# Mixer data in idle places of the raw-weight buffer, and layer 1's gate weights and column sums at other points of the program

## The chip, the cores and the metric

The kernel runs on one core of one Trainium2 chip. The metric is the device time of one execution in microseconds (us); lower is better. The kernel before takes 1125.44 us, the median of three runs (1125.43 to 1125.86).

## What is computed

A trunk of two layers on x of 512 tokens by 1024 channels, all in float32. Each layer is x + mixer(rmsnorm(x)), then x + mlp(rmsnorm(x)); a last rmsnorm ends the trunk. The MLP is `relu(h @ w1)**2 @ w2` with 4096 hidden channels.

- Layer 0's mixer has two halves. Differential attention: 4 heads, each with two softmaxes over 64-wide queries and keys, `p1 - lam * p2`, times v, normed per head. And pooling: 4 groups of 128 channels u, each `r = mean of the last w tokens - u` with w = 2, 4, 8, 16, times a 128x128 matrix. The eight results of 128 channels go through one output projection.
- Layer 1's mixer is gated linear attention, 4 heads with 128-wide keys and 256-wide values: `log_a = log_sigmoid(h @ w_low @ w_up + b) / 16` (the low rank is 16), a running sum of log_a per chunk gives the decays, then scores, state and output; the output is normed per head, multiplied by `silu(h @ w_g)` and projected.

## The kernel before

**Layout and matmuls.** Activations are kept with channels on the partitions: eight tiles of 128x512. A float32 product is made of three matmuls in a reduced format: a tensor is split into a high part (ScalarE, a copy) and a low part (VectorE, the difference), and hi x hi, lo x hi and hi x lo are added in one PSUM bank (L143 to L145, called by `proj_T`). `split_w` makes the two parts of a weight tile (L121 on ACT, L122 on DVE), `split_scaled` those of a normed activation (L175, L176), `split` those of a mixer's output (L181, L182). There are four buffers each for high and low weight parts, so a split waits until TensorE has read the tile four tiles before.

**Norms.** The norm's factor `rb` isn't applied ahead of a projection but behind it, when the result leaves PSUM. `Norm.add` adds the squares of the eight tiles (L232 on ACT, L241 on DVE); `col_sums` splits the sum (L197, L198) and adds over the partitions with two matmuls (L199, L200); `rsqrt` takes logarithm and exponential (L211, L212) and one Newton step (L204 to L206).

**Memory.** Weights come from HBM in loads of 1 MB into `raws`, 24 places of 512 columns: a ring of two loads (places 0 to 7) in the mixers, of five (0 to 19) in the MLPs, where places 20 to 23 hold a temporary `t2` of the weights. In layer 1's mixer places 8 to 11 hold states and 12 to 19 the values. Most other tensors are tiles of the pool `row` (54 of 128x512) or `tmp` (4). PSUM has eight banks under two tags, `mm` and `ax`, four each.

**Order.** A scheduler puts the instructions of each engine in a fixed order when the program is built, by priority (`soon()` raises it) and by when tiles come free. Engines then run in order and wait for each other by semaphores; all loads of weights are issued by SyncE (SP) in order too.

**Around the change.** In layer 0, q and k (L302), v (L355) and in layer 1 the gates g (L841) are rows. The pooling's u lies in two places of its own, with three more for its running sums (L398, L403). After layer 0's MLP, layer 1 begins: the low-rank gate weights `wgk` and the second gate matrix `wup` are loaded (L622, L624) and split (L637, L638, L641, L642); `psg` gathers the gate's column sums in 16 matmuls (L651), eight ahead of each half of head 0's q and k. Then `rb`; `gkf` (L659), its split (L660, L661), the second gate product for four heads (L665), `log_sigmoid` (L668 to L677, between two loads of ACT's tables, L674 and L679), running sums (L683), and head 0's q leaves PSUM (L699). At the mixer's end `gts` are taken through SiLU (L845), multiplied into the outputs (L846) and split (L181, L182) for the output projection (L421 adds its result to x).

Of the kernel before, what the change touches and what calls it, by code (L numbers as in the profile page):

```python
# [9 lines left out]
F32 = mybir.dt.float32  # L10
F32R = mybir.dt.float32r
U8 = mybir.dt.uint8
AF = mybir.ActivationFunctionType
ALU = mybir.AluOpType
AX = mybir.AxisListType

P = 128
S = 512
D = 1024
KB = D // P  # L20
# [15 lines left out]
def trunk(ctx: ExitStack, tc: tile.TileContext, xT, par, lvl, lam4, wqk0, wu0, wv0, poolw, wo0,  # L36
          wgk, wup, wqk1, wv1, wg1, wo1, w1a, w2a, w1b, w2b, gfin, out):
    nc = tc.nc
    V, A, G, PE = nc.vector, nc.scalar, nc.gpsimd, nc.tensor
# [10 lines left out]
    raws = T([P, 24 * S], "wraw", 1)  # L50
    ring = {}

    def turn(name, bufs):
        ring[name] = ring.get(name, -1) + 1
        return ring[name] % bufs

    def row(n=S, dt=F32):
        return T([P, n], "row", 54, dt)

    row8 = row16 = tmp2 = row  # L60


    def row_u(sums=True):
        c0 = 8 * S + (2 + turn("us", 3) if sums else turn("u", 2)) * (16 + S)
        return raws[:, c0:c0 + 16 + S]

    def row_state():
# [3 lines left out]
    mlp = [False]  # L71

    def tmp(n=S, dt=F32):
        if not mlp[0] and turn("tmp", 3) == 2:
            return row(n, dt)
        return T([P, n], "tmp", 4, dt)

    def PS(tag, shape=(P, S)):
        cnt[0] += 1
        return pp.tile(list(shape), F32, tag=tag, bufs=4, name=f"ps{tag}_{cnt[0]}")  # L80
# [5 lines left out]
    def soon(n=300):  # L86
        return tc.high_priority(n)
# [173 lines left out]
    act = []  # L261
# [9 lines left out]
    for kb in range(KB):  # L271
        c = slice(kb * P, (kb + 1) * P)
# [24 lines left out]
    def qk_heads(h):  # L297
        for j in range(2):
            ps = ps0[j] if h == 0 else proj_T(st.next(), act)
            t = row8()  # L300
            with soon():
                V.tensor_tensor(t, ps, rb, ALU.mult)  # L302
            qk[h, j] = t
# [46 lines left out]
    def values():  # L350
        r0 = per_token(rb)
        for t, ps in enumerate(proj_tok(Stream(wv0), act)):
            vt = row8()
            with soon():
                A.activation(vt, ps, AF.Copy, scale=r0[:, t:t + 1])  # L355
            v.append(vt)
# [35 lines left out]
    for i, g in enumerate((3, 2, 1, 0)):  # L392
        w = POOL_W[g]
        ps = proj_T(st.next(), act)
        u = row_u(False)
        G.memset(u[:, 0:16], 0.0)
        with soon():
            V.tensor_tensor(u[:, 16:], ps, rb, ALU.mult)  # L398
        s, step = u, 1
        while step < w:  # L400
            s2 = row_u()
            G.memset(s2[:, 0:16], 0.0)
            V.tensor_tensor(s2[:, 16:], s[:, 16:], s[:, 16 - step:16 + S - step], ALU.add)  # L403
            s, step = s2, 2 * step
        r = tmp2()
        V.scalar_tensor_tensor(out=r[:, 16:], in0=s[:, 32:], scalar=1.0 / w, in1=u[:, 32:], op0=ALU.mult,
                               op1=ALU.subtract)
        V.tensor_tensor(r[:, 0:16], s[:, 16:32], prm[:, C_ICNT + 16 * g:C_ICNT + 16 * (g + 1)], ALU.mult)
        V.tensor_tensor(r[:, 0:16], r[:, 0:16], u[:, 16:32], ALU.subtract)
        psy = PS("ax")  # L410
        PE.matmul(psy, pw[:, g, :], r, start=True, stop=True)
        cat[NH + i] = split_scaled(psy, prm[:, C_PSC + g:C_PSC + g + 1], (row16(dt=F32R), row16(dt=F32R)))

    def add_out(arr, src, col):

        st = Stream(arr)
        n, nxt = Norm(), []
        for f in range(KB):
            ps = proj_T(st.next(), src)
            with soon():  # L420
                V.tensor_tensor(x[f], x[f], ps, ALU.add)  # L421
                nxt.append(split_scaled(x[f], prm[:, col + f:col + f + 1]))
            n.add(x[f])
        return nxt, n

    def ffn(w1, w2, act, nrm, col):

# [15 lines left out]
        for c in range(4):  # L443
# [85 lines left out]
            def gather(t, nh, ps, first=False):  # L529
                with soon():  # L530
                    if first and c == 0 and not final:
                        acc[t][nh] = row8()
                        A.activation(acc[t][nh], ps, AF.Copy)
                    else:
                        V.tensor_tensor(acc[t][nh], acc[t][nh], shaped(ps), ALU.add)
# [7 lines left out]
            for n, (ps, first, t0, nh) in enumerate(plan):  # L543
                if n + 2 < 7:
                    w.append(prep(n + 2))
                product(n, w[n], ps, first)
                for t in range(2):
                    gather(t0 + t, nh, ps[t], n in (0, 2, 3))
            if c < 3:
                product(6, w[6], X, False)  # L550
                for t in range(2):
                    gather(2 + t, 0, X[t], True)
# [65 lines left out]
        nc.sync.dma_start(lf, lvl[:, i * S:(i + 1) * S])  # L618
        V.tensor_copy(lv[:, 4 * i:4 * i + 4, :].rearrange("p a b -> p (a b)"), lf)
    act, nrm = ffn(w1a, w2a, act, nrm, C_MIX1)  # L620
    gkr = row().rearrange("p (k a c) -> p k a c", k=KB, a=4)
    nc.sync.dma_start(gkr, wgk)  # L622
    wur = row()[0:96, :]
    nc.sync.dma_start(wur, wup)  # L624
    mlp[0] = False


    with soon(800):
        smask = row8()
        G.memset(smask, 1.0)  # L630
        G.memset(smask.rearrange("p (c t) -> p c t", t=P)[:, :, 0:1], 0.0)


        gk2 = [row8(dt=F32R).rearrange("p (k a b) -> p k a b", k=4, a=4) for _ in range(2)]
        for i in range(2):
            src = gkr[:, 4 * i:4 * i + 4, :, :]
            A.activation(gk2[i][:, :, :, 0:16], src, AF.Copy)  # L637
            V.tensor_tensor(gk2[i][:, :, :, 16:32], src, gk2[i][:, :, :, 0:16].bitcast(F32), ALU.subtract)  # L638

        wu = row8(dt=F32R)  # L640
        A.activation(wu[0:96, :], wur[0:96, :], AF.Copy)  # L641
        V.tensor_tensor(wu[64:96, :], wur[64:96, :], wu[64:96, :].bitcast(F32), ALU.subtract)  # L642

    psg = PS("mm")
    st = Stream(wqk1)
    wq0 = [st.next(), st.next()]
    psq0 = [PS("mm"), PS("mm")]
    for kbs in ((4, 5, 6, 7), (0, 1, 2, 3)):
        for kb in kbs:
            for j in range(2):  # L650
                PE.matmul(psg, gk2[kb // 4][:, kb % 4, :, :].rearrange("p a b -> p (a b)"), act[kb][j],  # L651
                          start=kb == 4 and j == 0, stop=kb == 3 and j == 1)
        for j in range(2):
            proj_T(wq0[j], act, ps=psq0[j], kbs=kbs, first=4, last=3)
    rb = nrm.rb()

    gkf = tmp2()
    gkl = row8(dt=F32R)
# [117 lines left out]

    def values1(half):
        for t, ps in enumerate(proj_tok(vst, act)):
            vt = raws[:, (12 + 4 * half + t) * S:(13 + 4 * half + t) * S]
            with soon():  # L780
                A.activation(vt, ps, AF.Copy, scale=r1[:, t:t + 1])
            vv[t][half] = vt
# [53 lines left out]
    gts = []  # L836
    for f in range(KB):
        ps = proj_T(st.next(), act)
        gt = row8()
        with soon():  # L840
            V.tensor_tensor(gt, ps, rb, ALU.mult)  # L841
        gts.append(gt)
# [95 lines left out]
```

## Time and profile before

| | |
|---|---|
| median of three runs | 1125.44 us |
| profiled execution, its own time | 1124.67 us |
| its span | 1122.9 us |
| busy: TensorE / VectorE / ScalarE | 1077.9 / 827.7 / 530.9 us |
| longest waits of TensorE | 11.0 us at L651, 7.9 us at L143 (for L699), 4.9 us at L143 (for L181) |
| granted clock, mean | 0.985 |

The profile is of one execution; its times are us from the span's start. A busy TensorE is at work or has a matmul in its pipe: in an unbroken run matmuls of 512 columns start every 0.227 us though one lasts 0.39. A line number is that of the helper that issued the instruction, so that L143 stands for every projection.

### The profile page before, as it was taken

Reading aid. Unit: us, or ns where it says so; the run is one execution under the profiler, and the core shown is the slowest. Engines: PE = TensorE matmul, PEld = TensorE weight load, DVE = VectorE, ACT = ScalarE, POOL = GpSimd, SP = SyncE. Lnnn points to the kernel's source line nnn. Section 1 sums busy time; section 2 is a strip of 40 time slices with the busy share of each in tenths; the row PEclk is TensorE's granted clock in tenths of the full one; section 3 lists DMA queues with packets and bytes.
Section 4 is the critical chain, followed back from the end, with each engine's and each line's share of the span. In section 5 each row is a group of like instructions: output and inputs, shape, how many; then the busy total and the mean of one; then the engine's idle time right before and its main releaser. Section 6 shows DMA issues by size and latency. Waiting matters only on the chain.

```text
span 1122.9 us, 12904 instructions
## 1 busy us (share of the span) xinstructions
PE 1077.9 (96%) x4968; PEld 867.5 (77%) x4968; DVE 827.7 (74%) x1234; ACT 530.9 (47%) x884; POOL 2.1 (0%) x20
## 2 busy tenths in 40 slices
PE   7999979999999999997879999999999999999996
PEld 5676658888888888886657788878888888888885
DVE  7757657695596696698588977556697597596696
ACT  6444525554443453445364546454554453453453
POOL 0000000000000000000000000000000000000000
PEclk9999989999999999999889999999999999999998
DMA  7221133305305206103211224222304305306102
GB/s 251 95 85 66 42 118 132 113 1 188 113 1 207 93 1 225 37 8 122 75 38 38 76 76 151 79 109 76 113 19 182 118 1 187 113 1 217 45 1 76
DMA packets 17917, 103.52 MB, mean 92 GB/s; under 512 B 2016, under 2 KB 3040, under 8 KB 6208
## 3 DMA queue, kind: packets, MB, share of 16 engines
q1 hardware_dynamic: 17712, 102.67, 25.5%
q8 instruction: 39, 0.64, 0.2%
q14 instruction: 22, 0.18, 0.1%
q10 hardware_dynamic: 144, 0.03, 0.0%
HBM read 100.59 MB, written 2.10 MB: 91 GB/s over the span
## 4 chain that ended last, share of the span: by engine, by line
PE 92%; DVE 3%; ACT 3%; DMA 1%; issue 0%; SPq 0%; DVEq 0%; ACTq 0%
PE psmm L143 15%; PE psmm L144 15%; PE psmm L145 14%; PE psmm L525 6%; PE psmm L527 6%; PE psmm L526 6%; PE psax L143 3%; PE psax L145 3%; PE psax L144 3%; PE psax L525 3%; PE psax L527 3%; PE psax L526 2%; PE psmm L169 2%; PE psmm L167 2%; PE psmm L168 2%; PE psax L316 1%
## 5 line engine op out<-in xcount | busy, mean ns | idle before, releaser
L121 ACT ACTIVATE wh<-wraw 128x1024 fp32r<-128x1024 f32 x230 | 243.6, 1061 | 420.5 <-PE psmm L144 181.5
L122 DVE TENSOR_TENSOR wl<-wraw,wh 128x1024 fp32r<-128x1024 f32 x230 | 280.3, 1221 | 82.6 <-ACT wh L121 82.0
L143 PE MATMUL psmm<-row,wh 128*128 128x512 f32 x736 | 290.9, 398 | 20.9 <-ACT row L181 7.9
L144 PE MATMUL psmm<-row,wh 128*128 128x512 f32 x736 | 290.8, 396 | 0.7 <-DVE row L182 0.7
L145 PE MATMUL psmm<-row,wl 128*128 128x512 f32 x736 | 290.7, 396 | 0.0
L143 PEld LDWEIGHTS psmm<-row,wh 128*128 128x128 f32 x736 | 139.5, 190 | 54.3 <-ACT row L181 9.3
L144 PEld LDWEIGHTS psmm<-row,wh 128*128 128x128 f32 x736 | 140.0, 190 | 33.4 <-issue 3.4
L145 PEld LDWEIGHTS psmm<-row,wl 128*128 128x128 f32 x736 | 139.6, 190 | 30.6 <-issue 2.0
L525 PE MATMUL psmm<-wh,row 128*128 128x512 f32 x320 | 124.6, 389 | 0.0
L526 PE MATMUL psmm<-wh,row 128*128 128x512 f32 x320 | 124.5, 389 | 0.0
L527 PE MATMUL psmm<-wl,row 128*128 128x512 f32 x320 | 124.5, 389 | 0.0
L500 DVE TENSOR_TENSOR wraw<-wraw 128x1024 f32<-128x1024 f32 x64 | 77.1, 1216 | 0.3
L452 DVE TENSOR_TENSOR row<-row,row 128x512 fp32r<-128x512 f32 x112 | 74.8, 682 | 0.3 <-ACT row L451 0.3
L527 PEld LDWEIGHTS psmm<-wl,row 128*128 128x128 f32 x320 | 60.1, 188 | 12.6
L526 PEld LDWEIGHTS psmm<-wh,row 128*128 128x128 f32 x320 | 60.1, 188 | 12.4
L525 PEld LDWEIGHTS psmm<-wh,row 128*128 128x128 f32 x320 | 60.1, 188 | 12.4
L451 ACT ACTIVATE row<-row 128x512 fp32r<-128x512 f32 x112 | 65.7, 618 | 5.3 <-DVE row L478 5.3
L466 DVE SCALAR_TENSOR_TENSOR tmp<-psmm,rb 128x512 f32<-128x512 f32 x48 | 32.9, 685 | 45.7 <-PE psmm L145 45.7
L471 ACT ACTIVATE row<-tmp 128x256 f32<-128x256 f32 x128 | 45.8, 405 | 10.9 <-DVE tmp L466 10.6
L145 PE MATMUL psax<-row,wl 128*128 128x512 f32 x128 | 49.8, 389 | 0.0
L144 PE MATMUL psax<-row,wh 128*128 128x512 f32 x128 | 49.8, 389 | 0.0
L527 PE MATMUL psax<-wl,row 128*128 128x512 f32 x128 | 49.8, 389 | 0.0
(231 smaller groups left out, 1306.5 us busy)
## 6 DMA issues: line engine op xcount, KB each, us to landing
wraw<-in_w1a SPq DMA_DIRECT2D x16, 1024.0 KB, 4.8
wraw<-in_w2a SPq DMA_DIRECT2D x16, 1024.0 KB, 4.8
wraw<-in_w2b SPq DMA_DIRECT2D x16, 1024.0 KB, 4.8
wraw<-in_w1b SPq DMA_DIRECT2D x16, 1024.0 KB, 4.8
wraw<-in_wo SPq DMA_DIRECT2D x8, 1024.0 KB, 4.7
wraw<-in_wqk SPq DMA_DIRECT2D x7, 1024.0 KB, 4.8
wraw<-in_wv SPq DMA_DIRECT2D x6, 1024.0 KB, 4.7
wraw<-in_wg SPq DMA_DIRECT2D x4, 1024.0 KB, 4.8
```

The costliest lines, as they stand in the source:

```text
L121: A.activation(hi, src, AF.Copy)
L122: V.tensor_tensor(lo, src, hi.bitcast(F32), ALU.subtract)
L143: PE.matmul(ps, wh, ah, start=first, stop=False)
L144: PE.matmul(ps, wh, al, start=False, stop=False)
L145: PE.matmul(ps, wl, ah, start=False, stop=last)
L451: A.activation(hi, src, AF.Copy)
L452: V.tensor_tensor(lo, src, hi.bitcast(F32), ALU.subtract)
L471: A.activation(raw[name][:, j, :], r[:, th * 256:th * 256 + 256], AF.Square)
L500: V.tensor_tensor(out[k], in0[k], in1[k], ALU.subtract)
L525: PE.matmul(ps[t], hi, wh[:, cs], start=f, stop=False, skip_group_check=True)
L526: PE.matmul(ps[t], lo, wh[:, cs], start=False, stop=False, skip_group_check=True)
L527: PE.matmul(ps[t], hi, wl[:, cs], start=False, stop=l, skip_group_check=True)
```

## The change

Six things change; what is computed doesn't.

- A helper `spare(k)` names place k of `raws`. Layer 0's q and k go to places 8 to 15, v to 16 to 19; layer 1's gates to 12 to 19, each behind the values' last reader.
- Pooling's u and its running sums share one ring of three buffers behind place 20.
- In the mixers every second `tmp` is a row (before, every third).
- `constants()` loads and splits the gate weights within layer 0's MLP, ahead of its last product, with places 20 and 21 as landing place.
- The 16 matmuls of `psg` stand behind head 0's q and k instead of ahead of each half.
- `rb` of layer 1 is issued under `soon()`.

Lines move by 3 to 12: `proj_T` is at L146 to L148 in the changed kernel, `psg` at L664, `gkf` and its split at L671 to L673, the second gate product at L677, the logarithm's table load at L686, head 0's q at L711, gates at L853, SiLU at L857, splits at L184 and L185.

```diff
@@ -60,8 +60,11 @@
     row8 = row16 = tmp2 = row
 
 
-    def row_u(sums=True):
-        c0 = 8 * S + (2 + turn("us", 3) if sums else turn("u", 2)) * (16 + S)
+    def spare(k):
+        return raws[:, k * S:(k + 1) * S]
+
+    def row_u():
+        c0 = 20 * S + turn("u", 3) * (16 + S)
         return raws[:, c0:c0 + 16 + S]
 
     def row_state():
@@ -71,7 +74,7 @@
     mlp = [False]
 
     def tmp(n=S, dt=F32):
-        if not mlp[0] and turn("tmp", 3) == 2:
+        if not mlp[0] and turn("tmp", 2):
             return row(n, dt)
         return T([P, n], "tmp", 4, dt)
 
@@ -297,7 +300,7 @@
     def qk_heads(h):
         for j in range(2):
             ps = ps0[j] if h == 0 else proj_T(st.next(), act)
-            t = row8()
+            t = spare(8 + 2 * h + j)
             with soon():
                 V.tensor_tensor(t, ps, rb, ALU.mult)
             qk[h, j] = t
@@ -350,7 +353,7 @@
     def values():
         r0 = per_token(rb)
         for t, ps in enumerate(proj_tok(Stream(wv0), act)):
-            vt = row8()
+            vt = spare(16 + t)
             with soon():
                 A.activation(vt, ps, AF.Copy, scale=r0[:, t:t + 1])
             v.append(vt)
@@ -392,13 +395,14 @@
     for i, g in enumerate((3, 2, 1, 0)):
         w = POOL_W[g]
         ps = proj_T(st.next(), act)
-        u = row_u(False)
+        u = row_u()
         G.memset(u[:, 0:16], 0.0)
         with soon():
             V.tensor_tensor(u[:, 16:], ps, rb, ALU.mult)
-        s, step = u, 1
+        s, step, us = u, 1, [row_u(), row_u()]
         while step < w:
-            s2 = row_u()
+            s2 = us[0]
+            us.reverse()
             G.memset(s2[:, 0:16], 0.0)
             V.tensor_tensor(s2[:, 16:], s[:, 16:], s[:, 16 - step:16 + S - step], ALU.add)
             s, step = s2, 2 * step
@@ -422,6 +426,29 @@
                 nxt.append(split_scaled(x[f], prm[:, col + f:col + f + 1]))
             n.add(x[f])
         return nxt, n
+
+    consts1 = {}
+
+    def constants():
+
+        gkr, wur = spare(20).rearrange("p (k a c) -> p k a c", k=KB, a=4), spare(21)[0:96, :]
+        nc.sync.dma_start(gkr, wgk)
+        nc.sync.dma_start(wur, wup)
+        smask = row8()
+        G.memset(smask, 1.0)
+        G.memset(smask.rearrange("p (c t) -> p c t", t=P)[:, :, 0:1], 0.0)
+
+
+        gk2 = [row8(dt=F32R).rearrange("p (k a b) -> p k a b", k=4, a=4) for _ in range(2)]
+        for i in range(2):
+            src = gkr[:, 4 * i:4 * i + 4, :, :]
+            A.activation(gk2[i][:, :, :, 0:16], src, AF.Copy)
+            V.tensor_tensor(gk2[i][:, :, :, 16:32], src, gk2[i][:, :, :, 0:16].bitcast(F32), ALU.subtract)
+
+        wu = row8(dt=F32R)
+        A.activation(wu[0:96, :], wur[0:96, :], AF.Copy)
+        V.tensor_tensor(wu[64:96, :], wur[64:96, :], wu[64:96, :].bitcast(F32), ALU.subtract)
+        consts1.update(smask=smask, gk2=gk2, wu=wu)
 
     def ffn(w1, w2, act, nrm, col):
 
@@ -546,6 +573,8 @@
                 product(n, w[n], ps, first)
                 for t in range(2):
                     gather(t0 + t, nh, ps[t], n in (0, 2, 3))
+            if c == 3 and not final:
+                constants()
             if c < 3:
                 product(6, w[6], X, False)
                 for t in range(2):
@@ -618,41 +647,24 @@
         nc.sync.dma_start(lf, lvl[:, i * S:(i + 1) * S])
         V.tensor_copy(lv[:, 4 * i:4 * i + 4, :].rearrange("p a b -> p (a b)"), lf)
     act, nrm = ffn(w1a, w2a, act, nrm, C_MIX1)
-    gkr = row().rearrange("p (k a c) -> p k a c", k=KB, a=4)
-    nc.sync.dma_start(gkr, wgk)
-    wur = row()[0:96, :]
-    nc.sync.dma_start(wur, wup)
     mlp[0] = False
 
 
-    with soon(800):
-        smask = row8()
-        G.memset(smask, 1.0)
-        G.memset(smask.rearrange("p (c t) -> p c t", t=P)[:, :, 0:1], 0.0)
-
-
-        gk2 = [row8(dt=F32R).rearrange("p (k a b) -> p k a b", k=4, a=4) for _ in range(2)]
-        for i in range(2):
-            src = gkr[:, 4 * i:4 * i + 4, :, :]
-            A.activation(gk2[i][:, :, :, 0:16], src, AF.Copy)
-            V.tensor_tensor(gk2[i][:, :, :, 16:32], src, gk2[i][:, :, :, 0:16].bitcast(F32), ALU.subtract)
-
-        wu = row8(dt=F32R)
-        A.activation(wu[0:96, :], wur[0:96, :], AF.Copy)
-        V.tensor_tensor(wu[64:96, :], wur[64:96, :], wu[64:96, :].bitcast(F32), ALU.subtract)
-
-    psg = PS("mm")
+    smask, gk2, wu = consts1["smask"], consts1["gk2"], consts1["wu"]
     st = Stream(wqk1)
     wq0 = [st.next(), st.next()]
     psq0 = [PS("mm"), PS("mm")]
+
     for kbs in ((4, 5, 6, 7), (0, 1, 2, 3)):
-        for kb in kbs:
-            for j in range(2):
-                PE.matmul(psg, gk2[kb // 4][:, kb % 4, :, :].rearrange("p a b -> p (a b)"), act[kb][j],
-                          start=kb == 4 and j == 0, stop=kb == 3 and j == 1)
         for j in range(2):
             proj_T(wq0[j], act, ps=psq0[j], kbs=kbs, first=4, last=3)
-    rb = nrm.rb()
+    psg = PS("mm")
+    for kb in range(KB):
+        for j in range(2):
+            PE.matmul(psg, gk2[kb // 4][:, kb % 4, :, :].rearrange("p a b -> p (a b)"), act[kb][j],
+                      start=kb == 0 and j == 0, stop=kb == KB - 1 and j == 1)
+    with soon():
+        rb = nrm.rb()
 
     gkf = tmp2()
     gkl = row8(dt=F32R)
@@ -776,7 +788,7 @@
 
     def values1(half):
         for t, ps in enumerate(proj_tok(vst, act)):
-            vt = raws[:, (12 + 4 * half + t) * S:(13 + 4 * half + t) * S]
+            vt = spare(12 + 4 * half + t)
             with soon():
                 A.activation(vt, ps, AF.Copy, scale=r1[:, t:t + 1])
             vv[t][half] = vt
@@ -836,7 +848,7 @@
     gts = []
     for f in range(KB):
         ps = proj_T(st.next(), act)
-        gt = row8()
+        gt = spare(12 + f)
         with soon():
             V.tensor_tensor(gt, ps, rb, ALU.mult)
         gts.append(gt)
```

The order moves at three places. The first is TensorE at the start of layer 1 (`psax` L560 or L589: transposes that end layer 0's MLP; L651 or L664: the gate's column sums). Before:

```order
L560 MATMUL psax_4088<-par_62,row_2227 128x128
L560 MATMUL psax_4089<-par_62,row_2227 128x128
L651 MATMUL psmm_4154<-row_4028,row_4146 128x512 [waits DVE_49]
L651 MATMUL psmm_4154<-row_4029,row_4146 128x512
L651 MATMUL psmm_4154<-row_4040,row_4146 128x512
```

And in the change, L146 to L148 being head 0's q:

```order
L589 MATMUL psax_4091<-par_62,row_2213 128x128
L146 MATMUL psmm_4149<-row_4030,wh_4141 128x512 [waits Activation_49]
L589 MATMUL psax_4088<-par_62,row_2215 128x128 [waits DVE_49]
L589 MATMUL psax_4089<-par_62,row_2215 128x128
L589 MATMUL psax_4090<-par_62,row_2215 128x128
L589 MATMUL psax_4091<-par_62,row_2215 128x128
L147 MATMUL psmm_4149<-row_4031,wh_4141 128x512
L148 MATMUL psmm_4149<-row_4030,wl_4142 128x512
```

The gate's sums stood next behind the transposes; now head 0's q (`psmm_4149`) stands there, its first matmul among the transposes. The gate's sums come behind q and k, and the column sums of the norm behind the first matmuls of the next head's q (`psmm_4428`):

```order
L664 MATMUL psmm_4199<-row_4069,row_4003 128x512
L146 MATMUL psmm_4428<-row_4106,wh_4424 128x512
L147 MATMUL psmm_4428<-row_4107,wh_4424 128x512
L148 MATMUL psmm_4428<-row_4106,wl_4425 128x512
L146 MATMUL psmm_4428<-row_4115,wh_4424 128x512
L202 MATMUL psax_4217<-row_4218,onesr_77 128x512 [waits PE_49,Activation_49]
L147 MATMUL psmm_4428<-row_4116,wh_4424 128x512
L148 MATMUL psmm_4428<-row_4115,wl_4425 128x512
L203 MATMUL psax_4217<-tmp_4219,onesr_77 128x512 [waits DVE_49]
```

The second place is VectorE in the same stretch, from the last additions of squares (`nacc`) to the second gate product's input. Before:

```order
L241 SCALAR_TENSOR_TENSOR nacc_4032<-tmp_4117,nacc_4032 128x512 [waits DVE_49]
L241 SCALAR_TENSOR_TENSOR nacc_4032<-tmp_4126,nacc_4032 128x512 [waits DVE_49]
L241 SCALAR_TENSOR_TENSOR nacc_4032<-tmp_4135,nacc_4032 128x512 [waits DVE_49,Activation_49]
L198 SCALAR_TENSOR_TENSOR tmp_4233<-nacc_4032,tmp_4232 128x512 [waits Activation_49]
L122 TENSOR_TENSOR wl_4633<-wraw_61,wh_4632 128x1024 [waits DMAHW4_49,PE_49,Activation_49]
L122 TENSOR_TENSOR wl_4664<-wraw_61,wh_4663 128x1024 [waits PE_49,Activation_49]
L204 SCALAR_TENSOR_TENSOR row_4240<-psax_4231,rb_4230 128x512 [waits Activation_49]
L205 SCALAR_TENSOR_TENSOR row_4240<-row_4240,rb_4230 128x512 [waits DVE_49]
L206 SCALAR_TENSOR_TENSOR rb_4230<-row_4240,rb_4230 128x512 [waits DVE_49]
L659 TENSOR_TENSOR row_4244<-psmm_4154,rb_4230 96x512 [waits DVE_49]
L661 TENSOR_TENSOR row_4245<-row_4244,row_4245 32x512 [waits Activation_49]
```

And in the change (L244: addition of squares, L125: low part of a weight tile, L671 and L673: the gate):

```order
L244 SCALAR_TENSOR_TENSOR nacc_4034<-tmp_4110,nacc_4034 128x512 [waits DVE_49]
L244 SCALAR_TENSOR_TENSOR nacc_4034<-tmp_4119,nacc_4034 128x512 [waits DVE_49]
L125 TENSOR_TENSOR wl_4650<-wraw_61,wh_4649 128x1024 [waits PE_49,Activation_49]
L244 SCALAR_TENSOR_TENSOR nacc_4034<-tmp_4128,nacc_4034 128x512 [waits DVE_49]
L244 SCALAR_TENSOR_TENSOR nacc_4034<-tmp_4137,nacc_4034 128x512 [waits DVE_49]
L201 SCALAR_TENSOR_TENSOR tmp_4219<-nacc_4034,row_4218 128x512 [waits Activation_49]
L207 SCALAR_TENSOR_TENSOR row_4226<-psax_4217,rb_4216 128x512 [waits Activation_49]
L208 SCALAR_TENSOR_TENSOR row_4226<-row_4226,rb_4216 128x512 [waits DVE_49]
L209 SCALAR_TENSOR_TENSOR rb_4216<-row_4226,rb_4216 128x512 [waits DVE_49]
L671 TENSOR_TENSOR row_4230<-psmm_4199,rb_4216 96x512 [waits DVE_49,PE_49]
L125 TENSOR_TENSOR wl_4817<-wraw_61,wh_4816 128x1024 [waits DMAHW7_49,PE_49,Activation_49]
L673 TENSOR_TENSOR row_4231<-row_4230,row_4231 32x512 [waits Activation_49]
```

The two low parts of head 2's weights stood between the sums' split (L198) and `rb`; now they stand further up, the second of them (`wl_4650`) between the last additions of squares, and one of the values' weights (`wl_4817`) stands between the gate and its split.

The third place is VectorE at the gates' end. Before (L841: a gate leaves PSUM, L846: times the output, L182: low part of the product):

```order
L841 TENSOR_TENSOR row_5713<-psmm_5688,rb_4230 128x512 [waits PE_49]
L122 TENSOR_TENSOR wl_5877<-wraw_61,wh_5876 128x1024 [waits DVE_49,Activation_49]
L846 TENSOR_TENSOR row_5444<-row_5444,row_5713 128x512 [waits Activation_49]
L182 TENSOR_TENSOR row_5733<-row_5160,row_5732 128x512
L182 TENSOR_TENSOR row_5737<-row_5172,row_5736 128x512 [waits Activation_49]
L182 TENSOR_TENSOR row_5741<-row_5210,row_5740 128x512 [waits Activation_49]
```

And in the change (L853, L858, L185):

```order
L185 TENSOR_TENSOR row_5731<-row_5380,row_5730 128x512 [waits Activation_49]
L853 TENSOR_TENSOR wraw_61<-psmm_5637,rb_4216 128x512 [waits PE_49]
L125 TENSOR_TENSOR wl_5818<-wraw_61,wh_5817 128x1024 [waits DMAHW2_49,Activation_49]
L858 TENSOR_TENSOR row_5418<-row_5418,wraw_61 128x512 [waits Activation_49]
L185 TENSOR_TENSOR row_5735<-row_5418,row_5734 128x512 [waits Activation_49]
L853 TENSOR_TENSOR wraw_61<-psmm_5667,rb_4216 128x512 [waits PE_49]
L125 TENSOR_TENSOR wl_5855<-wraw_61,wh_5854 128x1024 [waits Activation_49]
L858 TENSOR_TENSOR row_5430<-row_5430,wraw_61 128x512 [waits Activation_49]
L185 TENSOR_TENSOR row_5739<-row_5430,row_5738 128x512 [waits Activation_49]
```

The low parts stood in one run of eight behind the last gate; now each stands behind its own gate.

## Rows read from the trace of the kernel before

**Rows 1.** Page, parts 1 and 5: busy time of engines; two groups, mean ns of one.
```profile
PE 1077.9 (96%) x4968; PEld 867.5 (77%) x4968; DVE 827.7 (74%) x1234; ACT 530.9 (47%) x884; POOL 2.1 (0%) x20
...
L121 ACT ACTIVATE wh<-wraw 128x1024 fp32r<-128x1024 f32 x230 | 243.6, 1061 | 420.5 <-PE psmm L144 181.5
L122 DVE TENSOR_TENSOR wl<-wraw,wh 128x1024 fp32r<-128x1024 f32 x230 | 280.3, 1221 | 82.6 <-ACT wh L121 82.0
```

**Rows 2.** Waits of TensorE: engine, line, waited for: us in total, times, longest.
```profile
PE psmm L651 <- DVE row L638: 11.0, 1, 11.0
PE psmm L143 <- ACT row L181: 7.9, 3, 4.9
PE psmm L143 <- DVE row L699: 7.9, 1, 7.9
...
PE psmm L167 <- ACT wraw L781: 0.2, 1, 0.2
```

**Rows 3.** Timeline of PE, 524 to 576: start, us, line, op, xcount, [idle before <- releaser].
```profile
524.41 2.11 PE L560 MATMUL psax<-par,row 128*128 128x128 f32 x16
537.48 3.43 PE L651 MATMUL psmm<-row,row 128*128 128x512 f32 x8 [10.96 <-DVE row L638]
...
546.23 1.98 PE L651 MATMUL psmm<-row,row 128*128 128x512 f32 x8
...
553.71 0.39 PE L200 MATMUL psax<-tmp,onesr 128*128 128x512 f32 x1
...
560.00 1.19 PE L665 MATMUL psax<-row,row 96*128 96x512 f32 x4
...
566.37 0.39 PE L145 MATMUL psmm<-row,wl 128*128 128x512 f32 x1
574.62 0.80 PE L143 MATMUL psmm<-row,wh 128*128 128x512 f32 x1 [7.86 <-DVE row L699]
```

**Rows 4.** Timeline of DVE, 524 to 576.
```profile
532.83 0.74 DVE L176 SCALAR_TENSOR_TENSOR row<-x,par,row 128x512 fp32r<-128x512 f32 x1
...
541.08 0.69 DVE L198 SCALAR_TENSOR_TENSOR tmp<-nacc,tmp 128x512 fp32r<-128x512 f32 x1 [0.70 <-ACT tmp L197]
...
557.87 0.69 DVE L659 TENSOR_TENSOR row<-psmm,rb 96x512 f32<-96x512 f32 x1
...
573.90 0.66 DVE L699 SCALAR_TENSOR_TENSOR row<-psmm,rb 128x512 f32<-128x512 f32 x1
```

**Rows 5.** Windows: stretch, length, busy us of each engine, PEclk, DMA share, GB/s.
```profile
525.00:550.00 25.00, 14.04 (x62) 11.31 (x60) 15.63 (x24) 9.49 (x17) 0.00 (x0) 0.80 0.13 47
```

**Rows 6.** Timeline of ACT, 524 to 576.
```profile
560.53 1.27 ACT L668 ACTIVATE tmp<-psax,par 128x512 f32<-128x512 f32 x2
...
565.05 1.28 ACT L674 ACT_TABLE_LOAD   x1
```

**Rows 7.** DMA issues by line: KB each, median us to landing.
```profile
row<-in_wgk SPq DMA_DIRECT2D x1, 256.0 KB, 5.5
```

**Rows 8.** Timelines of PE, ACT and DVE, 727 to 748.
```profile
736.88 0.39 PE L145 MATMUL psmm<-row,wl 128*128 128x512 f32 x1
738.77 1.20 PE L143 MATMUL psmm<-row,wh 128*128 128x512 f32 x4 [1.50 <-ACT row L181]
...
746.44 0.39 PE L145 MATMUL psmm<-row,wl 128*128 128x512 f32 x1
...
738.62 0.62 ACT L845 ACTIVATE row<-row 128x512 f32<-128x512 f32 x1
739.26 1.28 ACT L848 ACT_TABLE_LOAD   x1
740.55 3.76 ACT L181 ACTIVATE row<-row 128x512 fp32r<-128x512 f32 x7
...
737.31 0.69 DVE L841 TENSOR_TENSOR row<-psmm,rb 128x512 f32<-128x512 f32 x1 [2.69 <-PE psmm L145]
```

**Rows 9.** Timeline of PE, layer 0's tail.
```profile
149.53 0.79 PE L143 MATMUL psmm<-row,wh 128*128 128x512 f32 x1 [4.91 <-ACT row L181]
```

## The prediction

> **What bounds the kernel now.** I read the engines' busy times first. TensorE is busy for 1077.9 of 1122.9 us [rows 1]: no other engine is near it, and the change removes no matmul, so all it can win is TensorE's 45.0 us of idle time, less the head and the tail of the program. The second view, TensorE's waits, tells where that time lies: one wait of 11.0 us for the split of the gate weights (L638), one of 7.9 us for an evacuation (L699), three of 7.9 us together for splits of activations (L181) [rows 2]. The first two lie in layer 1's first 50 us, the third is made of two waits in layer 0's tail and one at the end of the gates.
>
> Third, the timelines around each. At the layer boundary TensorE ends its transposes (L560) at 524.41 + 2.11 = 526.5 and restarts at 537.48 [rows 3], with half of the gate's column sums (L651), which stand ahead of the q,k products of head 0. The activations of those products lie ready from 533.6: the last L176 starts at 532.83 and takes 0.74 [rows 4]. The restart is slow: its 8 matmuls take 3.43 us, (3.43 - 0.39)/7 = 0.43 apart; the same 8 at 546.23 take 1.98, 0.227 apart [rows 3]. The granted clock of that stretch is 0.80 in the mean [rows 5], part of it at 1.2 and part at 2.4 GHz. Between 574.62 and the gates' end the longest wait left in the list is 0.2 us [rows 2], so what comes earlier at 575 stays earlier.
>
> **The change, part by part.** Sums go against the profiled execution, 1124.67 us, 0.77 under the median of 1125.44 shown; that 0.77 is added at the end.
>
> *1. Layer boundary.* What ends the second wait is a chain. In the kernel before: column sums of the squares on TensorE (the last, L200, at 553.71), inverse root, L659 at 557.87 [rows 4], L665 at 560.00, ACT's L668 from 560.53 and a table load at 565.05 [rows 6], logarithms, scans, L699 at 573.90 [rows 4], which frees the PSUM bank for which TensorE waits from 566.76 (566.37 + 0.39) to 574.62 [rows 3]. The first link was late only because of TensorE's order: DVE had the sums' input ready at 541.77 (541.08 + 0.69 [rows 4]), and TensorE came to it 12 us later.
>
> Now in the order of the change. TensorE takes the q,k products as activations come; the last comes about 533.6 and 16 matmuls of it remain, so both products end about 537.2, the 16 gate sums 16 x 0.227 = 3.6 later, 540.8. That is 12.5 us ahead of before, where the same work ended just ahead of the two column sums, at 553.5. The squares' chain on DVE now lets two weight splits (1.22 each [rows 1]) stand between its adds, where before it had the gate weights' three operations; it ends about 541.0, and hi and lo of the sum are there at 542.6. The second column sum (L203 of the changed kernel) starts at 542.65 where L200 started at 553.71: 11.1 ahead. Then two new links appear. ACT's split of a weight of the values (1.06 [rows 1]) stands ahead of L672 (L660 in before) and waits for TensorE to finish with a buffer (about 547.0); DVE's half of it (1.22) stands ahead of L673. So L673 starts about 549.4 and the gate's second product, L677, at 550.2, where L665 started at 560.00: 9.8 ahead. At the end of ACT's row a second weight split (1.06) has moved ahead of the table load: 8.7 ahead. From there to L711 (L699 in before) the order is that of before, so TensorE resumes at 574.62 - 8.7 = 565.9. **Gain 8.7 us.** The 11.0 us wait goes, and the second wait grows from 7.9 to about 11: its work is done earlier than the chain. What is late next is still that chain, ACT and DVE with TensorE idle. Bounds: 6.5, if the two weight splits hold the chain for a further 1.06 + 1.22 us, and 11.1, if they cost it nothing; I take 8.7 since the order puts each split in the chain's own queue.
>
> The loads of the gate weights (5.5 us to landing [rows 7]) move into layer 0's MLP; on SP's queue they now stand ahead of three loads of q,k weights, on DVE some 15 operations lie between the one that frees their place and the first that reads them, at 0.7 us or more each, so they land in time. Three DVE operations (L638 twice and L642, 1.5 us) and three ACT ones go with them. TensorE's products hide them, with DVE idle for a quarter of the time [rows 1]; without that cover they would cost their 1.5 us.
>
> *2. End of the gates.* In before the eight outputs' splits (L181, L182) run as one row after the gates: the last seven on ACT take from 740.55 to 744.31 [rows 8]. TensorE's last gate matmul starts at 736.88, and 29 matmuls have started by 746.44. At 0.227 they would take 6.6 us; they took 746.67 - 737.11 = 9.56, so 3.0 us are lost. In the change seven of the eight splits run during the gates, one beside each gate product, since a gate's place is no longer a row. Only the eighth is on the path: evacuation 737.31 + 0.69, ACT's SiLU 0.62, DVE's product, the table load 1.28, hi 0.6 and lo 0.7 give about 741.4 (times as in before). TensorE reads it after 21 matmuls, at 737.11 + 4.77 = 741.9. **Gain 2.9 us**; bounds 0.5 (a late eighth split by 2.4 us) and 3.0.
>
> The Trainium skill (ScalarE: Activation LUTs, section What ACT_TABLE_LOAD costs) says that a switch of tables costs a drain of about 1.38 us beside the load's 1.28, which speaks against this step: by it the eighth split would be at 742.8 and TensorE would wait 0.9 us, a gain of 2.0. The trace has the load at 739.26 and the next operation at 740.55, with nothing between [rows 8]; I go by the row.
>
> *3. Layer 0's tail.* The three u buffers are now shared with the running sums, so a group's u can be evacuated only when the group before it is done with its difference. The second product's 9 first matmuls of the output projection, which filled a wait in before, now need a bank that this evacuation frees; they run after the wait of 4.91 us that ends at 149.53 [rows 9]: 9 x 0.227 = 2.0 us lost if the wait stays. Against that, nine column-sum matmuls run earlier, and two of the sums' additions leave DVE's chain, so the wait can end up to 2.0 earlier. Bounds -2.0 and +1.0; **I take a loss of 0.5 us**, near the middle, as nothing in the rows ranks the two.
>
> *4. Start.* One addition of squares (about 0.7 us, as L198, of the same size [rows 4]) moves behind the last split: **a loss of 0.2 us**, between 0 and 0.7. The places of q, k, v and gates themselves cost nothing: same instructions, other addresses. The weight loads that now wait for those places are asked for tens of us later, so a landing like that of [rows 7] hides.
>
> Sum: 8.7 + 2.9 - 0.5 - 0.2 = 10.9. 1124.67 - 10.9 = 1113.8; with 0.77, **1114.5 us**.
>
> **The rivals.**
> *The chain eats more.* If the splits hold the gate chain to its lower bound (6.5) and the eighth split is late (0.5), with the same tail: 6.5 + 0.5 - 0.7 = 6.3, so 1119.1. For it: each of them waits for TensorE's reads, and ACT and DVE run in order. Against it: TensorE's last reads come about 547.0 and 554.4, just when the chain gets there.
> *The chain is freer.* 11.1 + 3.0 with no loss: 14.1, so 1111.3. For it: the sums are ready 11 us ahead. Against it: the two splits stand in the order.
> *Slower: the clock stays low from 528 on.* TensorE now gets the q,k products in pieces, as activations come, and not in one run. If the granted clock stays at 1.2 GHz through them, each matmul costs 0.2 us more (0.43 - 0.227). Place: the products before the gate sums and after. With 24 + 16 slow ones the sums end at 551 and the chain starts where it did in before: gain 0 there, 2.2 in all, 1123.2. If the next 36 are slow too, L677 comes 30 x 0.43 behind the column sums, about 567, 7 us late: 7 - 2.2 = 4.8 lost, 1130.2. It decides from some 55 slow matmuls on. Against it: after the rest of 10.96 us, 8 matmuls were enough to come back [rows 3].
> *The boundary's wait only moves.* If the chain hung on the squares and not on TensorE's order, 11 us would turn up again at 566. The row of L198, ready 12 us before its matmul, speaks against it [rows 3, 4]; the gain would be 2.2 and the time 1123.2, as above.
>
> **How the numbers follow.** The forecast's case (1112.5 to 1117) has 0.58, the chain that eats more (to 1120) 0.20, the freer chain (1110.8 to 1112.5) 0.10, the two that give 1123.2 0.07 together, of which half lies within 0.2% (2.25 us, about what can be told from no change), the slower one 0.05. The range 1111 to 1119.5 takes in the first, most of the second and of the third: 0.83. Faster by over 0.2%: 0.58 + 0.20 + 0.10 + 0.03 = 0.91; within: 0.04; slower: 0.05.
>
> **What would show it.** In the profile after: no wait at the gate sums; q,k products starting by 528; one wait of 10 to 12 us at the evacuation of head 0 (L711), ending near 566; ACT's table load near 556.4; no burst of splits after the gates and TensorE without a wait near 728. The prediction is wrong if the table load comes after 560, if the granted clock between 525 and 550 isn't over 0.8, or if layer 0's tail waits more than 7 us in all.

## The result and the profile after

The changed kernel takes 1115.24 us (median of four runs, 1114.37 to 1115.9) against 1125.43: 0.9909 of the time, 95% interval 0.9892 to 0.9926. The forecast was 1114.5. The profiled execution has a span of 1113.5 us where the one before had 1122.9, 9.4 us less; the steps summed to 10.9.

TensorE's busy time is the same, its idle time is not. From the first part of the changed kernel's page:

```profile
PE 1077.3 (97%) x4968; PEld 867.4 (78%) x4968; DVE 828.8 (74%) x1234; ACT 531.3 (48%) x884; POOL 2.3 (0%) x20
```

And from the view of TensorE's waits (us in total, times, longest):

```profile
PE psmm L146 <- DVE row L711: 11.1, 1, 11.1
PE psmm L146 <- ACT wh L270: 5.6, 2, 4.8
PE psmm L146 <- ACT row L184: 5.5, 2, 4.9
PE psax L202 <- ACT row L200: 4.4, 3, 2.5
```

The 11.0 us wait for the split gate weights of [rows 2] is gone, the 7.9 us wait for head 0's evacuation (now L711) has grown to 11.1, and one of the three waits for splits (L181, now L184) is missing: the one behind the gates. Within the last line hides a new wait of 1.23 us, which comes back below. The timeline of TensorE at the layer boundary, to be laid beside [rows 3]:

```profile
526.02 1.47 PE L589 MATMUL psax<-par,row 128*128 128x128 f32 x12
...
538.71 3.79 PE L664 MATMUL psmm<-row,row 128*128 128x512 f32 x16
...
544.10 0.42 PE L203 MATMUL psax<-tmp,onesr 128*128 128x512 f32 x1
...
551.74 1.09 PE L677 MATMUL psax<-row,row 96*128 96x512 f32 x4
...
567.20 0.79 PE L146 MATMUL psmm<-row,wh 128*128 128x512 f32 x1 [11.07 <-DVE row L711]
```

Between the transposes and the gate's sums stand 48 matmuls of q and k without a gap, at full speed: the first row below, a window of the changed kernel, has a granted clock of 1.00 (2.4 GHz) where [rows 5] had 0.80. It is the next stretch, with the 11 us wait, that has 0.80 now:

```profile
525.00:550.00 25.00, 24.78 (x117) 20.03 (x116) 21.22 (x30) 15.02 (x22) 0.00 (x0) 1.00 0.26 93
550.00:575.00 25.00, 13.93 (x56) 10.30 (x54) 19.74 (x31) 13.01 (x21) 0.00 (x0) 0.80 0.11 42
```

ScalarE's timeline (beside [rows 6]) has the two weight splits (L124) in the chain, ahead of the gate's split (which starts at 549.40) and ahead of the table load:

```profile
548.44 1.06 ACT L124 ACTIVATE wh<-wraw 128x1024 fp32r<-128x1024 f32 x1 [2.61 <-PE psmm L147]
...
552.17 1.27 ACT L680 ACTIVATE tmp<-psax,par 128x512 f32<-128x512 f32 x2 [2.15 <-PE psax L677]
...
556.03 1.07 ACT L124 ACTIVATE wh<-wraw 128x1024 fp32r<-128x1024 f32 x1
...
557.63 1.28 ACT L686 ACT_TABLE_LOAD   x1
```

At the gates' end (beside [rows 8]) VectorE evacuates the last gate, in its timeline:

```profile
731.06 0.69 DVE L853 TENSOR_TENSOR wraw<-psmm,rb 128x512 f32<-128x512 f32 x1 [1.31 <-PE psmm L148]
```

Behind it ScalarE has only the eighth split left, and TensorE goes on without a wait. ScalarE's timeline:

```profile
732.49 1.28 ACT L860 ACT_TABLE_LOAD   x1
733.84 0.63 ACT L184 ACTIVATE row<-row 128x512 fp32r<-128x512 f32 x1
```

**Where the lead was won and lost.** The same operation of VectorE, found in both traces, tells how far the changed kernel is ahead (-) or behind (+) at that place. The last column is the difference from the row above: what the stage between the two places won.

| place | before | after | lead | won in the stage |
|---|---|---|---|---|
| last x of layer 0's MLP (L564, L593) | 530.43 | 532.05 | +1.62 | -1.62 |
| head 0's q leaves PSUM (L699, L711) | 573.90 | 566.49 | -7.41 | 9.03 |
| head 1's q leaves PSUM (same lines) | 592.35 | 587.37 | -4.98 | -2.43 |
| last gate leaves PSUM (L841, L853) | 737.31 | 731.06 | -6.25 | 1.27 |
| last x of the projection (L421, L425) | 783.81 | 774.58 | -9.23 | 2.98 |

From there to the end of the span the lead stays, -9.20 at VectorE's last sums of the MLP and 9.4 at the end.

### The profile page after: what moved, and what is told of

It reads as the page before. It is cut to its first block, busy times and chain, and to the rows that moved or that the text cites. A ratio compares the mean times of both kernels' runs of the same rounds, so it can differ in the third digit from the quotient of the medians.

```text
span 1113.5 us, 12893 instructions
## 1 busy us (share of the span) xinstructions
PE 1077.3 (97%) x4968; PEld 867.4 (78%) x4968; DVE 828.8 (74%) x1234; ACT 531.3 (48%) x884; POOL 2.3 (0%) x20
## 4 chain that ended last, share of the span: by engine, by line
PE 93%; DVE 3%; ACT 2%; DMA 1%; issue 0%; SPq 0%; DVEq 0%
PE psmm L146 15%; PE psmm L147 14%; PE psmm L148 14%; PE psmm L554 6%; PE psmm L553 6%; PE psmm L552 6%; PE psax L148 3%; PE psax L147 3%; PE psax L146 3%; PE psax L554 3%; PE psax L552 3%; PE psax L553 3%; PE psmm L170 2%; PE psmm L172 2%; PE psmm L171 2%; PE psax L319 1%
## 5 line engine op out<-in xcount | busy, mean ns | idle before, releaser
L124 ACT ACTIVATE wh<-wraw 128x1024 fp32r<-128x1024 f32 x230 | 243.6, 1061 | 405.4 <-PE psmm L147 169.5
L125 DVE TENSOR_TENSOR wl<-wraw,wh 128x1024 fp32r<-128x1024 f32 x230 | 280.4, 1221 | 68.3 <-ACT wh L124 67.5
L146 PE MATMUL psmm<-row,wh 128*128 128x512 f32 x736 | 292.3, 398 | 22.7 <-DVE row L711 11.1
L148 PE MATMUL psmm<-row,wl 128*128 128x512 f32 x736 | 290.1, 395 | 0.0
L146 PEld LDWEIGHTS psmm<-row,wh 128*128 128x128 f32 x736 | 139.8, 190 | 56.0 <-DVE row L711 11.5
L148 PEld LDWEIGHTS psmm<-row,wl 128*128 128x128 f32 x736 | 139.6, 190 | 31.4 <-issue 2.6
L498 ACT ACTIVATE row<-tmp 128x256 f32<-128x256 f32 x128 | 45.8, 405 | 10.9 <-DVE tmp L493 10.6
L148 PE MATMUL psax<-row,wl 128*128 128x512 f32 x128 | 49.8, 389 | 0.0
L146 PE MATMUL psax<-row,wh 128*128 128x512 f32 x128 | 49.8, 389 | 0.0
L147 PE MATMUL psax<-row,wh 128*128 128x512 f32 x128 | 49.8, 389 | 0.0
```

What stands on the lines that cost most here:

```text
L124: A.activation(hi, src, AF.Copy)
L125: V.tensor_tensor(lo, src, hi.bitcast(F32), ALU.subtract)
L146: PE.matmul(ps, wh, ah, start=first, stop=False)
L147: PE.matmul(ps, wh, al, start=False, stop=False)
L148: PE.matmul(ps, wl, ah, start=False, stop=last)
L498: A.activation(raw[name][:, j, :], r[:, th * 256:th * 256 + 256], AF.Square)
```

## The experiments

Eleven kernels, in three groups, each group on one chip beside runs of the kernel before (1126.5, 1126.1 and 1126.3 us there). The changed kernel wasn't run again there, so it is compared by its ratio to the kernel before, 0.9909 (0.9892 to 0.9926). Spans and places are those of one profile of each kernel; the spans of one kernel's executions differ by 1 to 3 us.

**1. Sums ahead again, weights early.** The gate's sums go back to their old place in the changed kernel.

```diff
     for kbs in ((4, 5, 6, 7), (0, 1, 2, 3)):
+        for kb in kbs:
+            for j in range(2):
+                PE.matmul(psg, ...)
         for j in range(2):
             proj_T(wq0[j], act, ps=psq0[j], kbs=kbs, first=4, last=3)
...
```

> The changed kernel with the gate's column sums put back ahead of each half of head 0's q and k, the gate weights still loaded and split in layer 0's MLP. My theory: the 11.0 us wait was a wait for the split weights alone; with those ready 20 us earlier the sums only wait for activations like q and k do, so the place of the sums is worth nothing by itself: 1115 us, within 1.5, no wait over 2 us at the sums. Rival: the place of the sums made the gain at the boundary (9 us), and with them ahead TensorE comes late to the squares' column sums again: 1124.

Measured: 1113.72 us, 0.9888 (0.9874 to 0.9903). The wait of 11 us doesn't come back, so early weights are enough. And the place of the sums isn't neutral. The ratios of the two kernels overlap, but the stage can be told apart in the profiles: TensorE's wait at head 0's evacuation ends 3.3 us earlier than in the changed kernel, and the table load is at 554.36 instead of 557.63. The weight splits that stood between VectorE's last additions of squares and ahead of the gate's split now fall into gaps of the chain. Counted from the last x of layer 0's MLP, the boundary wins 12.0 us here and 9.0 in the changed kernel: with the weights early, the later place of the sums costs 3.0 there (2.2 between experiments 5 and 8, which differ by the same edit: 10.0 and 12.2). TensorE's timeline in this kernel:

```profile
563.93 0.79 PE L146 MATMUL psmm<-row,wh 128*128 128x512 f32 x1 [8.20 <-DVE row L710]
...
587.02 0.50 PE L170 MATMUL psmm<-wh,row 128*128 128x512 f32 x1 [1.17 <-DVE row L710]
```

The second row is where part of the lead goes again: at head 1's evacuation the lead has shrunk from 10.7 to 6.1 us.

**2. Only the sums moved, in the kernel before.** The same edit the other way round, with loads and splits of the gate weights left behind the MLP.

> The kernel before with one part of the change alone: the gate's column sums behind head 0's q and k, everything else as before (gate weights loaded and split behind the MLP). My theory: either part alone removes the 11.0 us wait, since the split weights are there at 537.4 us and q and k end about then; the three split operations then stand in the squares' chain on VectorE, so a little is lost: the wait at head 0's evacuation ends about 567, 1118 us (1116 to 1120). Rival: the early load is what counts, and the sums wait for the weights wherever they stand: 1123 to 1125.

Measured: 1117.34 us, 0.992 (0.9906 to 0.9935), span 1115.0: 7.9 us of the 9.4 with one edit. The sums wait 0.31 us for the weights instead of 10.96:

```profile
538.02 3.92 PE L654 MATMUL psmm<-row,row 128*128 128x512 f32 x16 [0.31 <-DVE row L638]
...
565.76 0.80 PE L143 MATMUL psmm<-row,wh 128*128 128x512 f32 x1 [9.21 <-DVE row L700]
```

So the two edits do the same thing twice: early weights, or other work ahead of the late ones. Either one alone removes the wait.

**3. Gates in rows.**

```diff
-        gt = spare(12 + f)
+        gt = row8()
```

> The changed kernel with the gates alone back in rows. My theory: at the end of the gates the eight splits run as one burst again because their row tiles come free only then, and 3.0 us come back: 1118.2 us, with waits of TensorE for the splits right behind the last gate matmul. Rival: the rows that q, k and v no longer hold are enough by then, and the splits stay beside the gates: 1115.2, no such wait.

Measured: 1118.95 us, 0.9937 (0.9922 to 0.9952). The waits of [rows 8] are back, 1.50 and 0.75 us, and the lead that was 5.5 us at the last gate is 5.7 at the end, where the changed kernel wins 3.0 in between.

**4. Head 0's q and k out of PSUM early.**

```diff
+    q0k0 = [row8(), row8()]
+    with soon():
+        V.scalar_tensor_tensor(out=q0k0[0], in0=psq0[0], scalar=float(P) ** -0.5, in1=rb, op0=ALU.mult, op1=ALU.mult)
+        V.tensor_tensor(q0k0[1], psq0[1], rb, ALU.mult)
     gkf = tmp2()
...
```

Head 0 then takes these two tiles instead of evacuating the banks itself.

> The changed kernel with head 0's q and k taken out of PSUM right behind the norm's factor, ahead of the gate chain, instead of behind the running sums. My theory: TensorE waits 11 us for a PSUM bank only, not for data; with the banks free it does head 2's q and k (48 matmuls, 10.9 us) in that time, and what follows needs those matmuls no more: 1106 to 1109 us, the chain itself about 1.4 us later. Rival: VectorE bounds the stage behind (128 of 162 us busy) and the wait comes back there: 1113 to 1115.

Measured: 1116.18 us, 0.9909 (0.9893 to 0.9926). My theory fell. The 11 us wait is gone and seven new ones stand behind it, of which the four longest are here, in TensorE's timeline:

```profile
570.21 0.58 PE L741 MATMUL psax<-par,tmp 128*128 128x128 f32 x3 [3.14 <-DVE tmp L738]
572.51 0.79 PE L202 MATMUL psax<-tmp,onesr 128*128 128x512 f32 x1 [1.73 <-ACT tmp L200]
...
578.20 0.61 PE L771 MATMUL psax<-row 128*32 128x32 f32 x8 [1.87 <-DVE row L764]
...
585.55 2.05 PE L778 MATMUL psax<-tmp 128*128 128x128 f32 x8 [1.80 <-DVE tmp L764]
```

With the wait of 1.21 us and two short ones they come to 10.7 us. Head 2's q and k were the only other work TensorE had beside head 0's scores; done earlier, they are missing later. From the squares to head 0's scores the chain, most of it on VectorE and ScalarE, sets the pace, and TensorE's idle time is what the chain leaves, wherever it is put. This fits the boundary's gain, which was the chain's 9 us and not the removed wait's 11. It isn't shown free of the clock: with the gaps the granted clock was 0.53 from 570 to 580 us and 0.50 from 580 to 590, where the changed kernel has 1.00 from 575 to 595, and the chain's own matmuls ran at 1.2 GHz. What that cost wasn't separated.

**5. Every third tmp a row.** The change has every second.

```diff
-        if not mlp[0] and turn("tmp", 2):
+        if not mlp[0] and turn("tmp", 3) == 2:
```

> The changed kernel with every third instead of every second tmp a row in the mixers, as in the kernel before. In the changed kernel 1.2 us of the lead are lost between head 0's evacuation and the gates, with a new wait of 1.2 us at a column sum of head 0 (588.69 us). Theory A: the other alternation of tmp buffers made the scheduler put VectorE's work in another order there; with it undone the lead holds: 1114.0 us, no such wait. Theory B: TensorE, which comes 7.4 us earlier, has run out of other matmuls while head 0's chain on VectorE is as long as before; the tmp buffers don't matter: 1115.2, the wait stays.

Measured: 1112.38 us, 0.9871 (0.9855 to 0.9888). Theory A. The wait at 588.69 us is gone, and the lead at the four heads' evacuations is 9.41, 9.21, 9.20 and 9.22 us: only 0.2 us is lost behind the boundary. The 3 us that this kernel's span is shorter are more than the 1.2 that theory A expected: its profile is also 1.1 us less late at the end of layer 0 and wins 0.9 more at the boundary.

**6. u in buffers of its own.**

```diff
-        return T([P, n], "row", 54, dt)
+        return T([P, n], "row", 52, dt)
...
-        u = row_u()
+        u = T([P, 16 + S], "uu", 2)
```

> The changed kernel with the pooling's u in two buffers of its own again (and two rows fewer in the pool), the running sums alone in the ring. Theory A: the shared ring of three, by holding the second u's evacuation back, costs the 0.9 us that the changed kernel loses between 120 and 170 us: 1114.3 us, and the second u is evacuated near 120 us again. Theory B: the loss is in the slower clock behind the wait of 4.9 us, which stays whatever the ring: 1115.2.

Measured: 1117.01 us, 0.9916 (0.9901 to 0.9931): by the ratio no different from the changed kernel. The second u is evacuated at 122 us again, but the profile is 3.9 us late at the end of layer 0. The two rows taken for u changed the order of the tail as well (a new wait of 3.13 us ends at 144.20), so this says nothing certain of the ring.

**7. The values' first splits out of the chain.**

```diff
...
+                with tc.issue_after(hold[0]):
+                    A.activation(hi, src, AF.Copy)
...
+    hold[0] = exps
     values1(0)
+    hold[0] = None
...
```

> The changed kernel with the splits of the values' first weights issued on ScalarE behind the second table load, out of the gate chain. My theory: each of the two stands in the chain on ScalarE and one on VectorE, together 2.4 us of it (the term between 11.1 and 8.7 us of the forecast): the table load comes 2.0 to 2.6 us earlier (near 555.3), head 0's evacuation ends TensorE's wait near 564.8, and the time is 1113 us. Rival: TensorE's products set the chain's pace there and the splits fit in gaps: 1115.2, the table load near 557.6.

Measured: 1114.67 us, 0.9896 (0.9881 to 0.9911). The chain is shorter as expected: TensorE's wait ends at 564.85 (8.89 us), the table load is at 555.27. The time is not clearly shorter: two waits of 1.39 and 1.01 us near 587 give it back, and head 1's evacuation is 4.8 us ahead, as in the changed kernel (5.0) and unlike experiment 5 (9.2).

**8 and 9. Both together.** Experiments 1 and 7, each with the edit of experiment 5. In the quoted expectations "the sixth" is experiment 5 here, and "the eighth" experiment 7.

> The changed kernel with both: the gate's column sums ahead (as the first experiment) and every third tmp a row (as the sixth). The sums ahead ended TensorE's wait 3.3 us earlier, but 2 us of that were lost again by head 1's evacuation; every third tmp kept the lead through that stage. My theory: the loss belongs to the order that the tmp buffers bring, so both gains add up: 1110 to 1111 us. Rival: head 0's chain allows no lead of more than some 9.2 us whatever the buffers: 1112.4, as the sixth alone.

> The changed kernel with the values' first splits behind the second table load (as the eighth) and every third tmp a row (as the sixth). My theory, as for the two apart: the chain is 2.2 us shorter and the lead isn't lost behind it: 1110 to 1111 us. Rival: no lead of more than 9.2 us lasts: 1112.4.

Measured: 1110.54 us, 0.9858 (0.9842 to 0.9875), and 1111.63 us, 0.987 (0.9856 to 0.9885). With the sums ahead the lead of 10.4 us at head 0 is 10.4 at head 1 and at the last gate: this kernel has the lowest time of all, though its interval overlaps the next ones'. With the late splits, 11.0 at head 0 falls to 9.8 at the last gate: more than the rival's 9.2 lasts, less than the theory's whole lead.

**10. Every second tmp a row, in the kernel before.** The edit of experiment 5 the other way round.

> The kernel before with one part of the change alone: every second instead of every third tmp a row in the mixers. My theory: this part alone costs time, 1 to 3 us, by the order of VectorE's work behind the gate chain and in layer 0: 1127 to 1129 by the 1126.1 of the kernel before on that chip. Rival: it only costs where the rest of the change has taken the waits away: within 1 us of the kernel before.

Measured: 1130.61 us, 1.0039 (1.0024 to 1.0054), more than I expected. It is 2.85 us late at the end of layer 0, 3.1 at head 0 and 5.0 at the last gate, with the same wait of 1.2 us for L699 at head 1 as in experiment 1.

**11. Gates in places of the raw weights, in the kernel before.**

```diff
-        gt = row8()
+        gt = raws[:, (12 + f) * S:(13 + f) * S]
```

> The kernel before with one part of the change alone: layer 1's gates in places 12 to 19 of the raw weights. My theory: the eight splits move beside the gates, 2.9 us less than the kernel before, no wait of TensorE behind the last gate matmul. Rival: the rows that q, k and v hold in layer 0 are needed too; the splits stay in one run, no difference.

Measured: 1123.19 us, 0.9974 (0.9964 to 0.9984). The span is 1120.4, 2.5 us less, after a start that was 0.4 late; TensorE's waits for splits fall from three (7.9 us) to two (6.3). From the last gate to the last x of the projection it wins 3.0, as the changed kernel does: the gates' place alone does it.

## Why the prediction was right, and where it was off

**The boundary** (forecast 8.7, measured 9.0). Every link came where the order put it, 1.6 us later by the start: gate sums at 538.71 (forecast 537.2 + 1.6), second column sum at 544.10 (542.65 + 1.6), second gate product at 551.74 (550.2 + 1.6), table load at 557.63 (556.4 + 1.6), TensorE's restart at 567.20 (565.9 + 1.6). The two weight splits in the chain cost what was taken off for them: without them the table load comes 2.2 us earlier (experiment 7, with the start's difference of 0.2 between the executions) where 2.4 were taken off, and 3.0 earlier in experiment 1 (0.3), whose additions of squares end earlier too. One subtraction on the way is off: 553.5 less 540.8 is 12.7, not 12.5; nothing rests on it.

**The gates' end** (forecast 2.9, measured 2.98; experiment 3, with gates in rows, is 5.5 us ahead at both ends of that stage). The load of ACT's table took 1.28 us here too, and the eighth split came behind it with 0.07 between. The drain that the Trainium skill (ScalarE: Activation LUTs, section What ACT_TABLE_LOAD costs) puts beside the load shows neither before nor after.

**Start and layer 0's tail** (forecast 0.7 lost, measured 1.6). Two terms of the tail came as forecast: nine fewer matmuls of TensorE stand ahead of the wait (543 instead of 552), and the wait, 4.91 us as before, ends 1.8 us earlier (147.75 instead of 149.53). What the sum leaves out is the clock. Five kernels have the changed layer 0 (the changed kernel and experiments 1, 3, 4 and 7). Behind that wait they run the same matmuls in the same order, first at 1.2 GHz. In the changed kernel and experiment 3 they need 384.3 and 384.4 us from there to the last x of the MLP, in experiments 1, 4 and 7 383.3 to 383.4: in the first two the clock comes back about 2 us later. So 1.0 us of the changed kernel's 1.6 is a difference between executions. The other three lose 0.7 to 1.0 us more than the changed kernel before the wait, which ends at 148.42 to 148.77 there. At the end of layer 0 the five are between 1.35 and 2.34 us late, 1.69 in the mean; experiments 2 and 11 have the layer 0 of before and are 0.46 and 0.42 late; all against the one profile of before. So 0.9 to 1.9 us may belong to the change, and single profiles settle it no closer. The three kernels with every third tmp a row (experiments 5, 8 and 9) are 0.54, 1.75 and 0.33 us late, 0.87 in the mean: about 0.8 us may belong to tmp, though the spread of single profiles is as large.

**Behind the boundary** (forecast nothing, measured 1.16 lost between head 0 and the gates). This is the step that failed: "what comes earlier at 575 stays earlier". TensorE was busy there without a gap in before, but with only 48 matmuls to spare beside a chain on VectorE, and the alternation of tmp, an edit that the prediction never priced, put head 1's evacuation (L711) further back in VectorE's order. VectorE's timeline in the changed kernel, where all three of head 0's masked copies of this kind (L771) stand ahead of it:

```profile
586.42 0.73 DVE L771 COPY_PREDICATED row<-lvl,psax 128x512 f32<-128x512 uint8 x1
587.37 0.68 DVE L711 SCALAR_TENSOR_TENSOR row<-psmm,rb 128x512 f32<-128x512 f32 x1
```

In experiment 5, as in before, only one of the three stands ahead of it:

```profile
583.14 0.68 DVE L711 SCALAR_TENSOR_TENSOR row<-psmm,rb 128x512 f32<-128x512 f32 x1
...
584.34 0.72 DVE L771 COPY_PREDICATED row<-lvl,psax 128x512 f32<-128x512 uint8 x1
```

And TensorE's timeline in the changed kernel has the new wait, which neither before nor experiment 5 has:

```profile
588.69 0.39 PE L202 MATMUL psax<-row,onesr 128*128 128x256 f32 x1 [1.23 <-ACT row L200]
```

Experiments 5 and 10 show that it is this edit. Which of the moved operations matters wasn't tried; the lead is 6.5 and 7.6 us at heads 2 and 3, so head 1's place can't be the whole account.

Sum: 9.0 + 3.0 - 1.6 - 1.2 = 9.2, and 0.2 at the very end.

**The rivals.** The clock didn't stay low: 1.00 in the window from 525 to 550. The boundary's wait did move in part, 3.2 us of the 11.0, as forecast, and didn't move whole. "The chain eats more" had 6.5 us at the boundary and "freer" 11.1, where 9.0 was measured.

## What to carry to other kernels

A wait of the busiest engine is worth what the chain behind its end gets shorter, not its length: here an 11.0 us wait was worth 9.0, and removing another of 11.1 us by reordering was worth nothing, in a stretch where the clock then stayed low as well. Two edits that remove the same wait don't add up, and one can cost time beside the other: with the weights early, the later sums did. Before counting on a lead that reaches a stage without gaps, look whether the engine is full there because it must be, or because it has a little other work to fill a chain's gaps. An edit that only changes which buffer a small tensor gets can still reorder an engine: price it by the scheduled order, or test it alone.

## What was not expected of the hardware

The granted clock's return after the same 4.91 us wait differed between executions of the same instructions. In the changed kernel and experiments 1, 3, 4 and 7 it was back at 1.00 (2.4 GHz) 7.3, 5.3, 7.5, 5.3 and 4.9 us behind the wait's end; in the window from 151 to 155 us it was 0.50, 0.66, 0.50, 0.61 and 0.69. That makes about 1 us of difference at the end of layer 0. Differences below that, in one profile each, say nothing.
